# Start of the out projection's operand, two recurrence pairs later, in a one-core transformer-layer kernel on Trainium2

## The chip, the core and the metric

The kernel runs on one core of one Trainium2 chip. The core's engines each run a queue of their own in order: TensorE (PE; its weight loads are listed apart as PEld), VectorE (DVE), ScalarE (ACT), GpSimd (POOL) and SyncE (SP). In this kernel SP issues nearly all DMA transfers; the transfers themselves run on 16 DMA engines shared by all queues. The metric is the device time of one execution in microseconds (us), as the median of several runs. One more execution is recorded by the hardware profiler; it has a time of its own.

## The reference

One layer on 2048 tokens of width 1024, all in fp32. Cut to what matters here:

```python
u = rms_norm(h, g_mix_pre)
z = u @ w_in                                     # 1024 -> 2816 columns
qa, ka, va, qh, fh, ih, gh = split(z)
ya = swa_with_sinks(qa, ka, va, sinks)           # sliding-window attention, 8 heads of 64
yh = hgrn2(qh, fh, ih, gh, lb, onorm)            # gated recurrence, 4 heads of 128
y  = concatenate([ya, yh]) @ w_out               # the out projection
h  = h + rms_norm(y, g_mix_post)
y  = cross_attention(rms_norm(h, g_x_pre), rms_norm(mem, g_mem), wq_x, wk_x, wv_x, wo_x)
h  = h + rms_norm(y, g_x_post)                   # mem: 256 tokens
y  = (silu(u @ w_gate) * (u @ w_up)) @ w_down    # u = rms_norm(h, g_ffn_pre)
h  = h + rms_norm(y, g_ffn_post)
```

## The kernel before, in words

**Arithmetic.** A matrix product in fp32 is made of three faster matmuls. Each operand is split in a high and a low part: ACT (or POOL) copies it to the rounded type (L987 in `split2`), DVE subtracts the copy from the original (L990). Then come high by high, high by low and low by high (L156 to L158 in `mm3`, L1131 to L1133 in `products`). So no weight can be used by PE before one load, one copy and one subtraction have ended.

**Stages.** `mix` (L194 on) holds the first quarter of the kernel. After a first block of the in projection it makes generators and calls `next` on them in turn, so that their work lies side by side:

- `cols` is the in projection of the second half of the tokens, one column of 128 outputs for each `next`: load the weights, split them, 48 matmuls of 128x512, an activation on ACT (L706, L708) and DVE (L713), and a store to `z_d`. The last four columns are those of the gate `gh`.
- `swa` is the attention, one pair of chunks (128 tokens) for each `next`; it writes `y_d`.
- `pairs` is the recurrence for pairs 8 to 15, staggered over ten yields: `hgrn_front` loads `k`, `qq`, `kk` and `v` from `z_d` and does the products L886, L897 and L902 (the last two are transposes on PE), `hgrn_state` carries the state `W` (L913, L915), `hgrn_out` (L925) loads the gate `sg` and makes the output, and `hgrn_last` stores it to `y_d`. The tile `v` has one buffer: the next pair's `v` is loaded when the transposes L902 of this one's have read it.
- `fold` is `fold_cross` (L272 on), in 32 steps. It first loads and normalises `mem` and transposes it (L124); then eight columns of wk, eight rows of wq (each result `x` is stored to `qk_d`), eight columns of wv, and wo in eight pieces (L348 to L350, results to `vo_d`). Each step loads 512 KB of weights into a tile `raw`, of which there are a few, and splits it on ACT and DVE into `whi` and `wlo`.
- `phases` runs the large products that follow, as a list of jobs. Job 0 is the out projection, with `w_out` as its operand `T` and `y_d` as the streamed operand `S` (tiles `sraw`). Its first eight steps are a prologue: each loads one half of a 512x512 block of `w_out`, 512 KB, into a tile `z` (two buffers, the same as those of the in projection's results) and splits it to `T` with one L987 and one L990 of 128x1024. Eight halves are the whole of `w_out`. The first products of job 0 follow when the fold has ended.

**Order.** The program fixes what depends on what; a scheduler that simulates the engines then decides the order within each engine's queue, starting from the order in which the work is written. `queued` (L438 on) restricts it: what is issued under it may not be put ahead of the instructions that it is given. `traced` (L433) finds the last instruction written so far for one engine.

**The place of the change.** Before, both last columns of the in projection are finished (L238 and L239) before the fold begins. Two fold steps follow. Then a loop takes the nine remaining yields of `pairs` (L245 to L249), with two fold steps after each, and from the second to the ninth it takes one half of `w_out` each. The last twelve fold steps (L250 and L251) stand alone.

Of the kernel before, what the change touches and what calls it, by code (L numbers as in the profile page):

```python
# [48 lines left out]
class Layer:  # L49
# [144 lines left out]
    def mix(self):  # L194
        tc, I = self.tc, self.I
        kw = dict(reuse_waits="tile")
        with contextlib.ExitStack() as left:
            def pool(name, at, **k):
                return at.enter_context(tc.tile_pool(name=name, bufs=1, **k, **kw))

            self.mc = pool("mc", left)
            self.r_x = self.cst.tile([P, NT], F32, name="r_x")
            with (
                tc.tile_pool(name="t1", bufs=3, **kw) as self.ts,
                tc.tile_pool(name="t2", bufs=3, **kw) as self.tb,
                tc.tile_pool(name="s1", bufs=2, side="right", **kw) as self.st_pool,
                contextlib.ExitStack() as at,
            ):
                self.banks(at, "ps1", **MOST)
                self.raws = 3  # L210
                u = self.in_first()
            self.banks(left, "ps2", **FOUR)
            self.hg = pool("hg", left)
            self.wp = pool("wp", left)
            self.io = pool("io", left)
            with tc.tile_pool(name="sw", bufs=1, side="right", **kw) as self.sw:
                self.zero_tiles()
                swa = self.swa(range(NT), lambda n: "st" if n < NPB else "sth")
                hgrn = self.hgrn(range(NPB), "h")
                cols = self.in_proj(1, u)  # L220
                next(cols)
                for _ in range(NPB + 1):
                    next(swa)
                    next(hgrn)
                    next(cols)
                for _ in hgrn:
                    pass
                self.out_sums, side = self.sums("out_s", self.w_out, 4, lambda: self.io_tile("u"), lambda: self.io_tile("x"))
                side = side()
                next(side)  # L230
                pairs = self.hgrn(range(NPB, NT), "gt")
                for i, _ in enumerate(swa, NPB + 2):
                    next(cols)
                    if i == NT + 1 - 0:
                        next(pairs)
                    for _ in range(4):
                        next(side, None)
                for _ in cols:  # L238
                    pass  # L239
            phases = self.phases(self.jobs(), None, lambda: self.io_tile("z"))  # L240
            with tc.tile_pool(name="xp", bufs=1, side="right", **kw) as self.xp:
                fold = self.fold_cross()
                for _ in range(2):
                    next(fold)
                for i, _ in enumerate(pairs, 1):  # L245
                    for _ in range(2):
                        next(fold)
                    if 2 <= i < 10:
                        next(phases)  # L249
                for _ in fold:  # L250
                    pass  # L251
            left.close()
            with (
                tc.tile_pool(name="t3", bufs=3, **kw) as self.ts,
                tc.tile_pool(name="t4", bufs=3, **kw) as self.tb,
                tc.tile_pool(name="s3", bufs=2, side="right", **kw) as self.st_pool,
                contextlib.ExitStack() as at,
            ):
                self.banks(at, "ps3", **MOST)
                self.raws = 4  # L260
                for _ in phases:
                    pass
# [1528 lines left out]
```

## Time and profile before

| | us |
|---|---|
| median of 3 runs | 2552.73 |
| lowest and highest run | 2552.61, 2555.01 |
| the profiled execution's own time | 2550.01 |
| its span (first to last instruction) | 2548.3 |
| PE busy | 2504.8 (98%) |
| DVE busy | 1792.1 (70%) |
| ACT busy | 1261.6 (50%) |
| POOL busy | 364.6 (14%) |

How to read it: the span is what the profile's rows divide up; the profiled execution's own time has 1.7 us more around it. An engine's busy time counts its instructions, not what it waits for. Groups and timelines name an instruction by engine, line, operation and `output<-inputs`; `[2.59 <-DMA v<-z_d]` behind a row says that the engine stood idle for 2.59 us before it and that a DMA into `v` from `z_d` ended the wait. An `x` and a number count instructions that a row stands for; matmuls overlap, so such a row's length is not their sum. Windows give the busy time of each engine in a stretch, then the TensorE clock that was granted (1.00 is full speed), the mean busy share of the 16 DMA engines and the bytes they moved; shares can come out slightly above 1.

### The profile page before, as it was taken

The numbers are of one execution on the slowest core, as the hardware profiler recorded it, in microseconds if no ns is written. First come the engines' busy times: TensorE is split into PE (matmuls) and PEld (weight loads), VectorE is DVE, ScalarE is ACT, GpSimd is POOL, SyncE is SP. The second block draws the span as 40 slices with busy tenths as digits, with TensorE's granted clock in tenths as the row PEclk, the third lists the DMA queues.
The fourth block names the chain that finished last, engine by engine and source line by source line (L and its number), as shares of the span: only waits on it lengthen the run. The fifth ranks groups of instructions, "written<-read, shape, count | busy, mean of one in ns | idle before, by whom it ended". The sixth has DMA issues, their size and how long they took to land.

```text
span 2548.3 us, 34324 instructions
## 1 busy us (share of the span) xinstructions
PE 2504.8 (98%) x12006; PEld 2092.8 (82%) x12006; DVE 1792.1 (70%) x2871; ACT 1261.6 (50%) x2635; POOL 364.6 (14%) x540
## 2 busy tenths in 40 slices
PE   9999999999999999999999999999999999999998
PEld 8878888877997778878878888888888888878886
DVE  8885488987556989988876555576566557574766
ACT  5553466655555566566753333353333335443543
POOL 4231234321311112102200000000000000000022
PEclk9999999999999999999999999999999999999999
DMA  6455655865887996867954522254465434564786
GB/s 201 146 165 178 192 154 170 230 204 146 259 292 275 316 335 189 274 206 226 333 200 146 177 91 87 74 203 148 160 210 195 144 117 159 180 188 106 228 177 151
DMA packets 387885, 486.33 MB, mean 191 GB/s; under 512 B 22272, under 2 KB 283392, under 8 KB 387712
## 3 DMA queue, kind: packets, MB, share of 16 engines
q1 hardware_dynamic: 381664, 462.12, 55.9%
q0 software_dynamic: 6048, 22.02, 5.0%
q8 instruction: 94, 1.54, 0.2%
q14 instruction: 79, 0.65, 0.1%
HBM read 317.34 MB, written 166.72 MB: 190 GB/s over the span
## 4 chain that ended last, share of the span: by engine, by line
PE 51%; DVE 2%; DMA 1%; issue 1%; ACT 1%; POOL 0%; SPq 0%; DVEq 0%; POOLq 0%; ACTq 0%
PE psm L1133 17%; PE psm L1131 17%; PE psm L1132 17%; DVE T L990 0%; DVE S L990 0%; ACT junk L1504 0%; PE pss L1390 0%; DMA out_dram<-row 0%; DMA row<-d_s 0%; DMA row<-in_w_down_dram 0%; DMA u_d<-row 0%; DMA sraw<-in_w_gate_dram 0%; DVE sum L1106 0%; ACT S L987 0%; ACT T L987 0%
## 5 line engine op out<-in xcount | busy, mean ns | idle before, releaser
L1131 PE MATMUL psm<-T,S 128*128 128x512 f32 x2680 | 1034.1, 390 | 13.3 <-ACT part L1146 7.2
L1132 PE MATMUL psm<-T,S 128*128 128x512 f32 x2680 | 1042.3, 390 | 4.0 <-DVE T L990 3.9
L1133 PE MATMUL psm<-T,S 128*128 128x512 f32 x2680 | 1029.4, 389 | 4.1 <-DVE S L990 4.1
L1131 PEld LDWEIGHTS psm<-T,S 128*128 128x128 f32 x2680 | 503.0, 188 | 125.9 <-ACT part L1146 11.9
L1132 PEld LDWEIGHTS psm<-T,S 128*128 128x128 f32 x2680 | 503.2, 188 | 110.5 <-DVE T L990 7.3
L1133 PEld LDWEIGHTS psm<-T,S 128*128 128x128 f32 x2680 | 503.1, 188 | 110.6 <-DVE S L990 6.3
L987 ACT ACTIVATE S<-sum 128x512 fp32r<-128x512 f32 (+1 forms) x370 | 224.0, 620 | 371.5 <-PE psm L1133 267.3
L990 DVE TENSOR_TENSOR S<-sraw,S 128x512 fp32r<-128x512 f32 (+1 forms) x315 | 211.5, 679 | 218.8 <-ACT S L987 215.8
L1146 ACT ACTIVATE part<-psm 128x512 f32<-128x512 f32 x285 | 168.6, 596 | 251.9 <-PE psm L1133 230.9
L990 DVE TENSOR_TENSOR S<-sum,S 128x512 fp32r<-128x512 f32 (+1 forms) x388 | 257.4, 673 | 42.1 <-ACT S L987 38.3
L987 ACT ACTIVATE S<-sraw 128x512 fp32r<-128x512 f32 (+1 forms) x300 | 184.7, 618 | 110.8 <-PE psm L1133 106.0
L1537 POOL DMA_DIRECT2D y_d<-row x16 | 14.1, 879 | 1077.9 <-DVE row L1721 1027.6
L990 DVE TENSOR_TENSOR T<-row,T 128x1024 fp32r<-128x1024 f32 (+1 forms) x112 | 131.0, 1183 | 30.2 <-ACT T L987 29.2
L157 PE MATMUL psg<-u,whi 128*128 128x512 f32 x320 | 128.3, 401 | 0.0
L158 PE MATMUL psg<-u,wlo 128*128 128x512 f32 x320 | 127.6, 399 | 0.0
L156 PE MATMUL psg<-u,whi 128*128 128x512 f32 x320 | 127.5, 399 | 0.0
L1504 ACT ACTIVATE junk<-row 128x512 f32<-128x512 f32 x160 | 99.6, 624 | 40.6 <-DVE row L1526 20.6
L987 ACT ACTIVATE T<-row 128x1024 fp32r<-128x1024 f32 (+1 forms) x112 | 113.3, 1031 | 7.5 <-DMA row<-d_s 4.3
L1672 DVE TENSOR_TENSOR row<-psm,part 128x512 f32<-128x512 f32 x66 | 43.7, 687 | 66.9 <-PE psm L1133 66.9
L1681 DVE TENSOR_TENSOR part<-psm,part 128x512 f32<-128x512 f32 x66 | 43.8, 687 | 60.1 <-PE psm L1133 59.8
L1721 DVE TENSOR_TENSOR row<-psm,part 128x512 f32<-128x512 f32 x72 | 49.1, 688 | 49.5 <-PE psm L1133 49.4
L814 ACT ACTIVATE S<-S,w_mn 128x256 f32<-128x256 f32 (+1 forms) x128 | 63.0, 496 | 29.6 <-DVE w_mn L810 29.2
(363 smaller groups left out, 3562.2 us busy)
## 6 DMA issues: line engine op xcount, KB each, us to landing
sraw<-in_w_gate_dram SPq DMA_DIRECT2D x44, 512.0 KB, 3.6
sraw<-in_w_up_dram SPq DMA_DIRECT2D x44, 512.0 KB, 3.7
hid_d<-row SPq DMA_DIRECT2D x44, 512.0 KB, 2.7
sraw<-hid_d SPq DMA_DIRECT2D x32, 512.0 KB, 4.2
sraw<-in_w_in_dram SPq DMA_DIRECT2D x44, 256.0 KB, 4.0
z_d<-pair SPq DMA_DIRECT2D x20, 512.0 KB, 3.4
raw<-in_w_in_dram SPq DMA_DIRECT2D x20, 512.0 KB, 4.8
z_d<-z SPq DMA_DIRECT2D x20, 512.0 KB, 4.0
```

The source lines that it names most:

```text
L156: nc.tensor.matmul(ps, ah, bh, start=(i == 0), stop=False)
L157: nc.tensor.matmul(ps, ah, bl, start=False, stop=False)
L158: nc.tensor.matmul(ps, al, bh, start=False, stop=(i == n - 1))
L814: nc.scalar.activation(s[:, r, o:], s[:, r, o:], AF.Exp, bias=mn[:, i:i + 1], scale=-1.0, accum_out=den[:, i:i + 1])
L987: self.nc.scalar.activation(hi, raw, AF.Copy)
L990: self.nc.vector.tensor_tensor(lo, raw, f32(hi), ALU.subtract)
L1131: nc.tensor.matmul(ps, s[:, 0, k, :], t[:, 0, k, :], start=st, stop=False, **kw)
L1132: nc.tensor.matmul(ps, s[:, 0, k, :], t[:, 1, k, :], start=False, stop=False, **kw)
L1133: nc.tensor.matmul(ps, s[:, 1, k, :], t[:, 0, k, :], start=False, stop=sp, **kw)
L1146: nc.scalar.activation(t, ps, AF.Copy)
L1504: self.nc.scalar.activation(junk, a, AF.Square, scale=float(D) ** -0.5, accum_out=to)
L1721: nc.vector.tensor_tensor(d, a, b, ALU.add)
```

## The change

It lies in `mix` alone:

```diff
-                for _ in cols:
-                    pass
             phases = self.phases(self.jobs(), None, lambda: self.io_tile("z"))
             with tc.tile_pool(name="xp", bufs=1, side="right", **kw) as self.xp:
                 fold = self.fold_cross()
-                for _ in range(2):
-                    next(fold)
+                engines = [getattr(mybir.EngineType, e) for e in ("SP", "Activation", "DVE")]
+                left_over = [0] * 8
+
+                def prologue():
+                    if left_over:
+                        left_over.pop()
+                        with self.queued(*(self.traced(e) for e in engines)):
+                            next(phases)
+
+                next(cols)
+                next(fold)
+                for _ in cols:
+                    pass
+                next(fold)
                 for i, _ in enumerate(pairs, 1):
                     for _ in range(2):
                         next(fold)
-                    if 2 <= i < 10:
-                        next(phases)
+                    if i >= 4:
+                        prologue()
                 for _ in fold:
-                    pass
+                    prologue()
+                assert not left_over
```

Three things differ. The halves of `w_out` are taken from the fourth to the ninth turn of the loop over the pairs (six of them), and after the first two of the twelve fold steps that follow (two more). Each half is written under `queued`, behind the last instruction written so far on SP, ACT and DVE. And the in projection's last column is written after the fold's first step (the memory's part and the first column of wk), no longer before it; the second-last column and the second fold step keep their places around them.

## The prediction, made before the changed kernel was run

> **What bounds the kernel now.** I began with the head of the page and the chain of waits.
>
> ```profile
> span 2548.3 us, 34324 instructions
> PE 2504.8 (98%) x12006; PEld 2092.8 (82%) x12006; DVE 1792.1 (70%) x2871; ACT 1261.6 (50%) x2635; POOL 364.6 (14%) x540
> ```
>
> PE is busy for 98% of the span, so 2548.3 − 2504.8 = 43.5 us of idle PE is all that a new order can win, plus whatever PE loses to a lower clock. The change adds and removes no arithmetic; it only moves work between about 590 and 774 us. So I asked for PE's waits in that stretch (line waiting, releaser: total us, times, longest).
>
> ```profile
> PE pst L902 <- DMA v<-z_d: 2.6, 1, 2.6
> PE pst L902 <- ACT whi L126: 1.1, 1, 1.1
> PE psh L849 <- DVE ptl L844: 1.0, 1, 1.0
> PE psg L897 <- DVE W L915: 0.8, 2, 0.5
> PE pst L925 <- ACT atz L888: 0.7, 1, 0.7
> PE pss L349 <- DVE wlo L990: 0.3, 1, 0.3
> PE pss L348 <- DVE kv L304: 0.2, 1, 0.2
> ```
>
> They add to 6.7 us. The largest is the load of `v` for the second pair; PE's timeline (start, us, instruction, idle before) and that of SP, which issues the loads in order, show why:
>
> ```profile
> 623.84 0.60 PE L902 MATMUL pst<-ident,v 128*128 128x128 f32 x4
> ...
> 630.78 1.04 PE L902 MATMUL pst<-ident,v 128*128 128x128 f32 x4 [2.59 <-DMA v<-z_d]
> 631.61 1.49 PE L886 MATMUL psg<-qq,k 128*128 128x192 f32 x4
> 633.21 1.09 PE L897 MATMUL psg<-ident,kk 128*128 128x128 f32 x4
> ...
> 645.88 0.81 PE L886 MATMUL psg<-qq,k 128*128 128x192 f32 x4
> 649.79 0.60 PE L897 MATMUL psg<-ident,kk 128*128 128x128 f32 x4
> ```
> ```profile
> 616.97 1.26 SPq L75 DMA_DIRECT2D z<-in_w_out_dram  x2
> ...
> 624.74 1.25 SPq L75 DMA_DIRECT2D z<-in_w_out_dram  x2
> 626.04 0.59 SPq L75 DMA_DIRECT2D v<-z_d  x1
> ```
>
> `v` has one buffer. It is free when the transposes of 623.84 are done (624.4), but SP first issues a half of `w_out` (two loads into `z`) and reaches `v` at 626.04. PE then stands for 2.59 us, and the same instructions take longer afterwards than at 645 to 650. The windows (length, busy us by engine, then granted clock, DMA share and GB/s) say the same, and show the fold's end:
>
> ```profile
> 630.00:640.00 10.00, 9.08 (x61) 8.23 (x62) 6.45 (x10) 6.47 (x18) 3.37 (x5) 0.83 0.98 281
> ```
> ```profile
> 725.00:735.00 10.00, 10.00 (x87) 10.00 (x86) 6.50 (x8) 7.01 (x17) 1.20 (x2) 1.00 0.83 258
> 735.00:745.00 10.00, 10.00 (x86) 10.00 (x86) 5.33 (x7) 3.58 (x6) 0.00 (x0) 1.00 1.08 346
> 745.00:755.00 10.00, 9.46 (x63) 8.00 (x62) 8.22 (x13) 7.78 (x13) 0.00 (x0) 1.00 1.04 398
> 755.00:765.00 10.00, 10.00 (x44) 7.84 (x43) 4.60 (x4) 7.19 (x11) 0.00 (x0) 1.00 0.98 347
> 765.00:775.00 10.00, 10.00 (x45) 8.08 (x44) 2.95 (x3) 5.90 (x10) 0.00 (x0) 1.00 0.51 204
> ```
>
> From 735 to 765 us the DMA engines are full while PE is fed without a gap worth naming. Two stretches, two limits: a load's place in SP's queue at 626 us, the rate of DMA at 735 to 765 us.
>
> **The moved halves, at their old place.** Eight halves of `w_out`, 512 KB each, are loaded (L75), copied by ACT (L987) and subtracted by DVE (L990):
>
> ```profile
> L75 SPq DMA_DIRECT2D z<-in_w_out_dram x12: 499/603/2971, 617.0 to 656.0; - x12
> L987 ACT ACTIVATE T<-z x8: 1057/1060/1063, 622.4 to 662.6; 128x1024 fp32r<-128x1024 f32 x8
> L990 DVE TENSOR_TENSOR T<-z,T x8: 1207/1226/1470, 623.5 to 664.2; 128x1024 fp32r<-128x1024 f32 x8
> ```
>
> In the changed order the second pair's `k`, `qq` and `v` follow each other on SP, and the loads of five more pairs come before the first half. So `v` can go at 624.4, not 626.04. How long it takes is read from the issues of 610 to 662 us (engine, form, count, size, median us to landing):
>
> ```profile
> z<-in_w_out_dram SPq DMA_DIRECT2D x4, 512.0 KB, 6.9
> k<-z_d SPq DMA_DIRECT2D x3, 256.0 KB, 4.0
> v<-z_d SPq DMA_DIRECT2D x3, 256.0 KB, 4.6
> ```
>
> 624.4 + 4.6 = 629.0; PE needs it at 630.78 − 2.59 = 628.2. That leaves a wait of 0.8 us; with `k`'s 4.0 it is 0.2. I take 0.6, since less is in the queue. Gain 2.0. The slow clock is worth (1.04 − 0.60) + (1.49 − 0.81) + (1.09 − 0.60) = 1.6 us, which the window's (1 − 0.83) × 9.08 = 1.5 confirms. I let this cost vanish with the long wait. First term: −3.6, bounds 0 (the single buffer keeps `v` as late as it is) and −4.2.
>
> [...]
>
> **ACT and DVE relieved.** From 622 to 664 us they lose 8 × 1.06 = 8.5 and 8 × 1.23 = 9.8 us of work. PE's waits on `atz`, `W` and `whi` (0.7 + 0.8 + 1.1 = 2.6 us) end on ACT or DVE; the rows don't say how many of them the splits caused, and I take a third. Second term −0.8, bounds −2.6 and +1.1: at their new place the splits can make one wait as long as the longest of these.
>
> **The last gate column beside the fold's first step.** Its 48 matmuls keep their engine and number; the memory's loads, norms and eight transposes come ahead of them. Its weights are loaded later, the first step's earlier. What lies at that place is the wait of 1.0 us on `ptl` (592 us), which neither load releases. Term 0; bounds −1.0 (the new neighbours fill it) and +2.6 (a weight late by as much as `v` was).
>
> **The halves at their new place.** By the changed order three halves go between the stores of wq's results, beside the last pairs, and five follow the last of wq's stores, two of them ahead of the last two wv columns, two between the loads of the first token blocks and one before the fifth piece of wo, in SP's queue:
>
> ```profile
> 734.02 0.57 SPq L78 DMA_DIRECT2D qk_d<-x  x1
> ...
> 743.20 5.02 SPq L75 DMA_DIRECT2D raw<-in_wo_x_dram  x2
> ```
> ```profile
> 754.51 0.50 PE L349 MATMUL pss<-wlo,kv 128*128 128x512 f32 x1 [0.29 <-DVE wlo L990]
> ...
> 774.30 0.39 PE L1131 MATMUL psm<-T,S 128*128 128x512 f32 x1
> ```
> ```profile
> 740.86 1.06 ACT L987 ACTIVATE whi<-raw 128x1024 fp32r<-128x1024 f32 x1 [1.60 <-DMA raw<-in_wv_x_dram]
> ...
> 765.23 1.06 ACT L987 ACTIVATE whi<-raw 128x1024 fp32r<-128x1024 f32 x1 [0.74 <-DMA raw<-in_wo_x_dram]
> ```
>
> The stretch from 725 to 765 moves (258 + 346 + 398 + 347) × 10 us = 13.5 MB; five halves add 2.62 MB. At its own mean, 337 GB/s, that takes 7.8 us more; if all of it ran at the 398 GB/s of its best window, 16.1 MB take 40.5 us and it costs 0.5. ACT already waits for `raw` at 740.86 and 765.23, and PE for `wlo` at 754.51, so the splits are just in time: the weights have perhaps 1 us to spare (765.23 + 1.06 + 1.23 = 767.5 against its use about two steps of (774.30 − 754.51) / 7 = 2.8 us before 774.30, that is 768.7). Nor is there room in SP's queue: a `z` buffer is busy for 6.9 + 1.06 + 1.23 = 9.2 us, so with two the third and fourth of the five can be issued only 9.2 us after 734, at 743 or later, where SP would hold back the wo loads of 743.20. I take +4.0, between 0.5 and 7.8, near the middle since rate and spare time both count. Five copies and five subtractions (5.3 and 6.1 us) fit into ACT's and DVE's idle time there, and cost nothing unless late data makes them stand ahead of `whi`. `T` itself isn't late: the last half is split before the wo pieces end, and PE first needs one at 774.30.
>
> [...]
>
> **Later jobs.** Their splits and waits change order only a little; what PE waits for from 774 to 1300 us:
>
> ```profile
> PE psm L1133 <- DVE S L990: 4.1, 4, 1.6
> PE psm L1131 <- ACT S L987: 3.9, 3, 1.7
> PE psm L1132 <- DVE T L990: 3.9, 6, 1.4
> ```
>
> 11.9 us in all; nothing says which way they go. Term 0, bounds ±2 (a sixth of it).
>
> **Sum.** −3.6 − 0.8 + 0 + 4.0 + 0 = −0.4 us. The profiled execution took 2550.01 us (1.7 around its span) and would take 2549.6; it is 2.7 below the median of the runs, 2552.73, so the median becomes 2552.3. About 0.2%, 5.1 us, is what a measurement of this kernel can tell from no change.
>
> **Rivals.**
> *The fold's end takes the halves without harm* (faster). For it: PE waited only 0.3 us at wo, DMA reached 398 GB/s, and after 765 us its share falls to 0.51. Against it: that room lies behind the last load PE waits for. The sum is then −3.6 − 0.8 + 0.5 = −3.9, and with the early terms most of the way to their bounds −4.2 − 1.7 − 0.5 = −6.4: 2546.3 to 2548.8, likely 2547.5.
>
> *The wo loads queue behind the halves and PE starves at the fold's end* (slower). One mechanism: from the moment a half waits for its `z` buffer on SP, each wo load behind it is late by the rest of the 9.2 us, and the DMA then works the 2.62 MB ahead of them. It decides if the waits at L349 and L350 (wo's matmuls) add to over 4 us. Price: 7.8 by DMA, about 2.5 for SP held from 743.2 (the third and fourth half's 0.6 us each and the landing of what follows them), 1.6 for a clock that falls as it did at 631; less 4.4 gained: +7.5, so 2560.2; from 2557 on where half of the queue's cost hides.
>
> *The stall doesn't go* (the change doesn't do what it says). `v`'s single buffer and a landing of over 6 us leave most of the 2.59 us and the slow clock; only 0.5 of the first term is gained: −0.5 − 0.8 + 4.0 = +2.7, 2555.4.
>
> **How the numbers follow.** My forecast, 2552.3, has a chance of 0.36, with an own range of 2549 to 2556; halves absorbed 0.25; starved 0.26; stall stays 0.13. Faster by over 5.1 us (below 2547.6): half of the absorbed case and a sliver more where the early stretch gives its bounds too, 0.21 in all. Slower by over 5.1 (above 2557.8): nine tenths of the starved case and a little of the last two, 0.28. Within: 0.51. The range reaches into both cases, 2546.5 to 2560.5, and leaves out some 0.07 below and 0.11 above.
>
> **What would show it.** Right: no wait on `v` over 1 us and a clock of 1.00 from 630 to 640; several new waits at L348 to L350 on `wlo` or `whi`, 3 to 5 us in all, with DMA full to nearly 770; job 0 beginning at about the time it began. If job 0 begins 4 us earlier, the tail absorbed the halves; if over 5 us later, it starved. Wrong altogether if PE's time changes after 1300 us, or between 590 and 620.

## The result, and the profile after

| | before | changed |
|---|---|---|
| median, us | 2552.67 (8 runs) | 2559.57 (8 runs) |
| lowest to highest | 2549.82 to 2555.01 | 2557.71 to 2562.35 |
| profiled execution, us (span) | 2550.01 (2548.3) | 2562.35 (2560.6) |

The ratio is 1.0028, with a 95% interval of 1.0019 to 1.0037: slower, by about 7 us. The profiled execution of the changed kernel is the longest of its eight, so the two profiles lie 12.3 us apart where the medians lie 6.9 apart. Of all the runs in this document one, of e7, took 3126.36 us at a granted clock of 0.752, where every other had at least 0.994, and e7's time below is the median of its other seven.

The head of the page and PE's waits of 0.5 us or more from 590 us to the start of job 0, of the changed kernel (behind `mix` its line numbers are 11 higher: L908 is L897 of before, L913 is L902, L359 is L348, L998 is L987, L1142 is L1131):

```profile
span 2560.6 us, 34333 instructions
...
PE 2509.6 (98%) x12006; PEld 2096.0 (82%) x12006; DVE 1792.5 (70%) x2871; ACT 1262.7 (49%) x2635; POOL 365.8 (14%) x540
```
```profile
PE psh L359 <- DVE kv L315: 2.9, 1, 2.9
PE pss L359 <- ACT whi L998: 2.6, 1, 2.6
PE pss L156 <- ACT whi L126: 1.9, 1, 1.9
PE pss L156 <- ACT whi L998: 1.3, 1, 1.3
PE pss L158 <- DVE wlo L1001: 0.8, 1, 0.8
PE pss L156 <- DVE mT L127: 0.7, 1, 0.7
PE pss L360 <- DVE wlo L1001: 0.5, 1, 0.5
PE psg L908 <- DVE W L926: 0.5, 1, 0.5
```

The wait on `v` is gone. The load of `v` goes out at 621.37, right behind the transposes of 620.74 that free its buffer (623.84 before), and the transposes of 626.35 find it there. All the long waits are new, and all end on ACT or DVE work that belongs mostly to the fold (L126 splits wq's rows, L314 and L315 copy and split a column of wv's result, L359 to L361 are wo's matmuls). To see when the time changes hands, take marks that both kernels pass in the same sequence: the transposes of `kk` of the first pair (at 590 us) and of the last one, and job 0's first matmul. PE's timeline of before and then of the changed kernel:

```profile
590.54 0.60 PE L897 MATMUL psg<-ident,kk 128*128 128x128 f32 x4
...
707.65 0.60 PE L897 MATMUL psg<-ident,kk 128*128 128x128 f32 x4
```
```profile
590.15 0.66 PE L908 MATMUL psg<-ident,kk 128*128 128x128 f32 x4 [0.27 <-ACT atz L899]
...
620.74 0.60 PE L913 MATMUL pst<-ident,v 128*128 128x128 f32 x4
...
626.35 0.60 PE L913 MATMUL pst<-ident,v 128*128 128x128 f32 x4
...
700.71 0.60 PE L908 MATMUL psg<-ident,kk 128*128 128x128 f32 x4
...
708.88 0.39 PE L156 MATMUL pss<-kv,whi 128*128 128x256 f32 x1 [1.89 <-ACT whi L126]
...
743.82 0.39 PE L156 MATMUL pss<-mT,whi 128*128 128x256 f32 x1 [1.27 <-ACT whi L998]
745.08 0.38 PE L158 MATMUL pss<-mT,wlo 128*128 128x256 f32 x1 [0.76 <-DVE wlo L1001]
...
755.87 0.50 PE L359 MATMUL psh<-whi,kv 128*128 128x512 f32 x1 [2.94 <-DVE kv L315]
759.39 0.80 PE L359 MATMUL pss<-whi,kv 128*128 128x512 f32 x1 [2.55 <-ACT whi L998]
771.65 0.50 PE L360 MATMUL pss<-wlo,kv 128*128 128x512 f32 x1 [0.52 <-DVE wlo L1001]
...
782.46 0.39 PE L1142 MATMUL psm<-T,S 128*128 128x512 f32 x1
```

The pairs' stretch (first to last `kk`) takes 707.65 − 590.54 = 117.1 us before and 110.6 after: 6.5 us gained. The fold's end (last `kk` to job 0) takes 774.30 − 707.65 = 66.7 before and 81.8 after: 15.1 us lost. Job 0 begins 8.2 us later than before, though the first mark was passed 0.4 us earlier.

The windows of the changed kernel (columns as before):

```profile
630.00:640.00 10.00, 10.00 (x86) 10.00 (x85) 5.66 (x8) 4.62 (x15) 4.33 (x5) 1.00 0.84 247
...
700.00:710.00 10.00, 7.77 (x66) 7.38 (x64) 3.98 (x7) 4.31 (x9) 1.14 (x2) 1.00 0.85 236
710.00:720.00 10.00, 10.00 (x73) 9.99 (x74) 4.88 (x8) 4.59 (x15) 1.93 (x3) 0.83 0.58 193
...
740.00:750.00 10.00, 7.97 (x65) 7.57 (x64) 7.71 (x10) 6.48 (x10) 0.00 (x0) 1.00 1.10 308
750.00:760.00 10.00, 4.50 (x21) 3.17 (x21) 5.94 (x9) 5.55 (x8) 0.00 (x0) 0.91 1.04 363
760.00:770.00 10.00, 10.00 (x35) 7.95 (x34) 4.10 (x4) 6.70 (x10) 0.00 (x0) 0.75 0.97 365
```

Where 630 to 640 us had a clock of 0.83 it now has 1.00 and a busy PE. But 700 to 710 and 740 to 760 have idle PE, and a slower clock follows each: 0.17 × 10.0 + 0.09 × 4.5 + 0.25 × 10.0 = 4.6 us, an estimate from the windows. The waits after 700.71 add 1.89 + 0.34 (a second one on `whi` at 710) + 1.27 + 0.76 + 2.94 + 2.55 + 0.52 = 10.3 us; before had 0.5 there. Together 10.3 + 4.6 − 0.5 = 14.4 of the 15.1 us.

Why PE waits is read from ACT, DVE and SP of the changed kernel:

```profile
707.29 1.06 ACT L998 ACTIVATE T<-z 128x1024 fp32r<-128x1024 f32 x1 [4.08 <-DMA z<-in_w_out_dram]
708.25 0.58 ACT L126 ACTIVATE whi<-pss 128x512 fp32r<-128x512 f32 x1
...
753.17 1.06 ACT L998 ACTIVATE T<-z 128x1024 fp32r<-128x1024 f32 x1 [0.95 <-DMA z<-in_w_out_dram]
754.13 0.37 ACT L314 ACTIVATE kv<-psh 128x256 fp32r<-128x256 f32 x1
...
758.28 1.06 ACT L998 ACTIVATE whi<-raw 128x1024 fp32r<-128x1024 f32 x1 [2.08 <-DMA raw<-in_wo_x_dram]
```
```profile
754.26 1.23 DVE L1001 TENSOR_TENSOR T<-z,T 128x1024 fp32r<-128x1024 f32 x1 [1.24 <-ACT T L998]
755.40 0.42 DVE L315 TENSOR_TENSOR kv<-psh,kv 128x256 fp32r<-128x256 f32 x1
```
```profile
732.27 0.34 SPq L78 DMA_DIRECT2D qk_d<-x  x1
732.66 2.27 SPq L75 DMA_DIRECT2D z<-in_w_out_dram  x3
...
735.62 1.76 SPq L75 DMA_DIRECT2D raw<-in_wv_x_dram  x2
...
741.84 2.74 SPq L75 DMA_DIRECT2D z<-in_w_out_dram  x3
...
746.45 4.97 SPq L75 DMA_DIRECT2D raw<-in_wo_x_dram  x3
```

Two things. At 707 us ACT stands 4.08 us for a half that hasn't landed, and the copy of `whi` (L126), for which PE waits, stands behind it on the same engine; at 753 it is the copy of `kv` (L314), and on DVE its subtraction (L315) stands behind that of the half. And on SP the halves are issued ahead of weights: the second load for wo goes at 746.45 (743.20 before), the fifth at 760.62 (754.49), and ACT waits for a wo load until 758.28. The DMA engines didn't make up for it. One window from wq's last store to job 0, before and then changed; both hold the same loads and stores, but for the five halves:

```profile
734.02:774.30 40.28, 39.74 (x238) 34.32 (x237) 20.61 (x25) 24.18 (x39) 0.00 (x0) 1.00 0.91 326
```
```profile
732.27:782.46 50.19, 42.14 (x232) 35.60 (x230) 27.78 (x32) 30.20 (x45) 0.00 (x0) 0.93 0.91 301
```

The share was 0.91 and stays so, and the stretch grew by 9.9 us. At the 326 GB/s of before the 2.62 MB of five halves alone are 8.0 us: they were paid with time.

### The profile page after: what moved, and what is told of

It is laid out like the page before. It is cut to its first block, busy times and chain, and to the rows that moved or that the text cites. A ratio compares the mean times of both kernels' runs of the same rounds, so it can differ in the third digit from the quotient of the medians.

```text
span 2560.6 us, 34333 instructions
## 1 busy us (share of the span) xinstructions
PE 2509.6 (98%) x12006; PEld 2096.0 (82%) x12006; DVE 1792.5 (70%) x2871; ACT 1262.7 (49%) x2635; POOL 365.8 (14%) x540
## 4 chain that ended last, share of the span: by engine, by line
PE 51%; DVE 2%; ACT 1%; issue 1%; DMA 1%; POOL 0%; SPq 0%; DVEq 0%; POOLq 0%; ACTq 0%
PE psm L1142 17%; PE psm L1144 17%; PE psm L1143 17%; DVE T L1001 1%; DVE S L1001 0%; ACT junk L1515 0%; PE pss L1401 0%; ACT T L998 0%; DMA row<-in_w_down_dram 0%; DMA out_dram<-row 0%; DMA row<-d_s 0%; DMA u_s<-row 0%; DVE sum L1117 0%; ACT S L998 0%; DVE row L1645 0%
## 5 line engine op out<-in xcount | busy, mean ns | idle before, releaser
L1142 PE MATMUL psm<-T,S 128*128 128x512 f32 x2680 | 1034.5, 391 | 14.5 <-ACT part L1157 7.3
L1142 PEld LDWEIGHTS psm<-T,S 128*128 128x128 f32 x2680 | 503.4, 188 | 127.5 <-ACT part L1157 11.9
L1144 PEld LDWEIGHTS psm<-T,S 128*128 128x128 f32 x2680 | 503.6, 188 | 112.3 <-DVE S L1001 8.1
L998 ACT ACTIVATE S<-sum 128x512 fp32r<-128x512 f32 (+1 forms) x370 | 223.8, 620 | 378.8 <-PE psm L1144 278.9
L998 ACT ACTIVATE S<-sraw 128x512 fp32r<-128x512 f32 (+1 forms) x300 | 184.8, 617 | 107.7 <-PE psm L1144 103.6
L998 ACT ACTIVATE T<-row 128x1024 fp32r<-128x1024 f32 (+1 forms) x112 | 113.3, 1030 | 7.7 <-DMA row<-d_s 4.8
L1526 POOL TENSOR_TENSOR q_v<-q_s 128x2 f32<-128x2 f32 x39 | 16.8, 431 | 426.0 <-ACT junk L1515 426.0
```

The costliest lines, as they stand in the source:

```text
L998: self.nc.scalar.activation(hi, raw, AF.Copy)
L1142: nc.tensor.matmul(ps, s[:, 0, k, :], t[:, 0, k, :], start=st, stop=False, **kw)
L1144: nc.tensor.matmul(ps, s[:, 1, k, :], t[:, 0, k, :], start=False, stop=sp, **kw)
```

## The experiments

Each ran five rounds against the kernel before. The table reads every kernel by the marks above (us, from each kernel's profiled execution): first to last `kk`, last `kk` to job 0, their sum, and job 0 to the end.

| | pairs | fold's end | sum | rest | ratio to before, 95% interval |
|---|---|---|---|---|---|
| before | 117.1 | 66.7 | 183.8 | 1774.0 | |
| changed | 110.6 | 81.8 | 192.3 | 1778.1 | 1.0028 [1.0019, 1.0037] |
| e1 column only | 119.7 | 69.4 | 189.1 | 1774.1 | 1.0005 [0.9995, 1.0015] |
| e2 halves only | 110.8 | 80.8 | 191.6 | 1782.9 | 1.0030 [1.0018, 1.0042] |
| e3 no load | 110.9 | 78.3 | 189.2 | 1777.7 | 1.0004 [0.9995, 1.0014] |
| e4 v, two buffers | 117.5 | 67.8 | 185.3 | 1778.0 | 0.9992 [0.9983, 1.0001] |
| e5 few bytes | 110.1 | 74.6 | 184.7 | 1778.2 | 0.9988 [0.9978, 0.9998] |
| e6 split later | 110.4 | 83.4 | 193.8 | 1775.0 | 1.0023 [1.0015, 1.0032] |
| e7 earlier in turn | 122.2 | 72.7 | 194.9 | 1779.4 | 1.0037 [1.0024, 1.0050] |
| e8 earlier, split later | 110.7 | 74.2 | 184.9 | 1773.6 | 1.0006 [0.9995, 1.0016] |
| e9 two per turn | 121.3 | 65.0 | 186.3 | 1773.5 | 1.0006 [0.9997, 1.0015] |
| e10 two, SP only | 119.6 | 68.7 | 188.3 | 1772.4 | 1.0006 [0.9998, 1.0015] |
| e11 two, old column | 122.1 | 66.4 | 188.4 | 1777.4 | 1.0015 [1.0006, 1.0024] |
| e12 mixed | 122.6 | 66.7 | 189.3 | 1776.7 | 1.0011 [1.0001, 1.0021] |

Three cautions for the table. The last time column scatters by itself: over these kernels it lies between 1772.4 and 1782.9 us, and e4, which differs from before only in a buffer of `v`, has 1778.0 where that has 1774.0. So 4 us between two profiles of that part tell nothing, and the changed kernel's +4.1 there isn't put down to the change. Next, a profile is one execution: e8's is the shortest of its eleven, 6.7 us below their median, those of e3 and of the changed kernel are their longest. What the sums say is therefore held against the ratios, which come from all runs; before's own median in these rounds lay between 2552.59 and 2554.86 us. Last, the marks part the same work in most kernels, but not in all. Between the first and the last `kk` PE has 793 to 797 matmuls in the others, 782 in e8, 810 and 811 in e9 and e11, and 826 in e12. At about 0.12 us for one of the fold's (an estimate from their spacing) some 1.7 us of the pairs' work is counted at the fold's end in e8; as much of the fold's end is counted among the pairs in e9 and e11, and 3.5 us of it in e12. The sums don't change by that.

**e1, column only.** The changed kernel without the queueing:

```diff
-                        with self.queued(*(self.traced(e) for e in engines)):
-                            next(phases)
+                        next(phases)
```

> The changed kernel without the queueing of the halves; the scheduler then loads them at their old place beside the second to fifth pairs (the order of all loads is that of a kernel in which only the last gate column is moved). If the loss comes from the halves at the fold's end (theory): 2550 to 2555 us, job 0 begins within 2 us of 774, the long wait on v is there again or smaller. If moving the column costs (rival): 2557 us or more, with new waits before 640 us.

2556.22 us against 2554.86, between the two expectations; job 0 begins at 778.6 us, later than the theory had it. The halves are loaded from 617 to 657 us, where the kernel before has them: writing them two turns later has no effect, and the queueing alone moves them. The stall stays and has another name. DVE and PE of this kernel:

```profile
629.82 0.17 DVE L287 TENSOR_SCALAR gx<-gx 128x8 f32<-128x8 f32 x1 [2.06 <-DMA gx<-in_g_x_pre_dram]
```
```profile
630.73 0.55 PE L156 MATMUL psh<-mT,whi 128*128 128x256 f32 x1 [2.47 <-DVE mT L127]
```

DVE stands for `gx`, a load of 4 KB, and the split `mT` behind it keeps PE waiting. The pairs' stretch is 119.7, the fold's end 69.4: nearly all of the loss at the fold's end belongs to the queued halves.

**e2, halves only.** Both last columns before the fold, as in the kernel before; the halves as changed:

```diff
+                for _ in cols:
+                    pass
             phases = self.phases(self.jobs(), None, lambda: self.io_tile("z"))
...
-                next(cols)
-                next(fold)
-                for _ in cols:
-                    pass
-                next(fold)
+                for _ in range(2):
+                    next(fold)
```

> The halves queued later as in the changed kernel, both gate columns before the fold as in the kernel before. Theory: 2557 to 2562 us, PE waits of 6 to 10 us in all between 740 and 775 us and one of some 2 us near 705, job 0 begins 6 to 9 us later than before. Rival (the column's move costs): 2553 us or less.

2562.38 us. 110.8 and 80.8 us, the changed kernel's stretches to within 1 us: the halves do all of it, the gain among the pairs too, and moving the column is worth nothing beside them.

**e3, no load.** From the third half on `get` in `phases` gives back one of the first two tiles and loads nothing, so `T` isn't `w_out`:

```diff
+                if tile is prologue and len(stale) >= 2:
+                    stale.append(0)
+                    return stale[len(stale) % 2][:, :c]
```

> The changed kernel with the loads of the third to eighth half left out: their copies and subtractions stay and read the tiles of the first two. If the 3 MB and the waits for them make the loss (theory): 2544 to 2548 us, no PE wait over 1 us between 740 and 775. If the copies and subtractions make it by their own time, standing between those of the fold (rival): 2555 us or more.

2556.32 us, as a time in the rival's range; but before had 2554.86 in these rounds, and a loss of 1.5 us is neither the theory's gain nor as much as the rival had. The second half is still loaded, ACT stands 5.26 us for it and PE 3.08; and with the loads gone the scheduler put token loads ahead of the last wv columns, where PE waits 2.38 us at 755 though no half is loaded there. The run doesn't separate the theories.

**e4, two buffers for v.** In the kernel before:

```diff
-        v = get(new("v"), C_IH)
+        v = get(new("v", 2), C_IH)
```

> The kernel before with a second buffer for v and nothing else changed. If the place of v's load behind the halves made the stall of 2.59 us and the slow clock after it: the wait on v is gone, 2548 to 2550 us. If the load is late for another reason (DMA full, the data not yet in memory): the wait stays or goes to another tile, 2551 to 2554 us.

0.9992, not clear of 1. PE's wait on `v` is gone, and the next transposes wait in its place:

```profile
626.61 0.49 PE L902 MATMUL pst<-ident,v 128*128 128x128 f32 x3
...
630.61 0.63 PE L897 MATMUL psg<-ident,kk 128*128 128x128 f32 x4 [2.86 <-issue]
```

117.5 us among the pairs, as before. So the single buffer of `v` was not what cost. What the next transposes wait for isn't shown: the row names no releaser, and SP issued their `kk` at 590 us already.

**e5, few bytes.** The changed kernel; the loads of the third to eighth half take 64 of 512 columns, so `T` isn't `w_out` here either:

```diff
+                if tile is prologue and len(stale) >= 2:
+                    t = stale[len(stale) % 2]
+                    stale.append(t)
+                    jobs[n][0](t[:, :c, 0:64], i, j, a, c, 64)
+                    return t[:, :c]
```

> The changed kernel with an eighth of the bytes in the loads of the third to eighth half (64 of 512 columns; the rest of T is made from stale data). The queueing, the copies and the subtractions stay. From the last product of wq to job 0 the kernel before takes 44.2 us, the changed one 54.9. If the bytes in the full DMA stretch make the loss (theory): 44 to 47 us, no wait over 1 us there, time within 3 us of before. If the place of the copies and subtractions in ACT's and DVE's order makes it (rival): 50 us or more.

2552.46 us, 0.9988: in the medians all of the loss is gone, and more. From wq's last product to job 0 it takes 47.2 us, at the edge of what the theory expected. The fold's end falls from 81.8 to 74.6 us with the copies and subtractions still there: about half of the 15.1 us goes with the bytes. ACT's standing for the last five halves (4.0 us in the changed kernel) goes with them, so this run alone doesn't part the two. What is left holds a PE wait of 3.07 us at 711, behind ACT's 5.25 us for the second half, which is loaded whole in this run; from 745 us on there remain waits of 1.92 and 0.38.

**e6, split later.** In the prologue each half is split after the next one's load is written:

```diff
                 half(-1, prologue)
-                split(len(steps))
+                if i:
+                    split(len(steps))
                 yield
+            split(len(steps))
```

> The changed kernel with each half's copy and subtraction written one half after its load, so that ACT need not stand still for the load; bytes and queueing stay. If ACT's standing in order for the halves, with the fold's copies behind it, makes most of the loss: the wait near 705 us gone, the stretch from wq's last product to job 0 at 46 to 49 us, 2550 to 2555 us. If the bytes alone make it: that stretch stays above 52 us and the time near 2558.

2559.81 us, 83.4 at the fold's end, 54.3 from wq's last product to job 0: the second branch of the expectation. ACT's standing for halves falls to 2.4 us in all (11.4 in the changed kernel), and nothing is won, because another load is late and another engine stands for it. DVE and PE:

```profile
725.26 0.75 DVE L955 SCALAR_TENSOR_TENSOR sg<-psg,onorm,sg 128x512 f32<-128x512 f32 x1 [3.79 <-DMA sg<-z_d]
```
```profile
726.66 0.58 PE L158 MATMUL psh<-kv,wlo 128*128 128x256 f32 x1 [4.06 <-DVE wlo L127]
```

**e7, earlier in the turn.** The changed kernel with one half in each of the first eight turns, ahead of the fold's two steps:

```diff
+                    if i >= 1:
+                        prologue()
                     for _ in range(2):
                         next(fold)
-                    if i >= 4:
-                        prologue()
```

> The halves still queued, but one in each of the first eight turns and ahead of the turn's two fold steps: the loads then stand one behind each pair's loads, from the second pair to the wv columns, and only the last is within the stretch of full DMA. If the full stretch makes the loss: wq's last product to job 0 in 44 to 47 us, 2546 to 2553 us. If a queued half costs wherever it stands (ACT in order for its load): waits of 1 to 3 us with a slower clock between 645 and 730, 2555 us or more.

2564.74 us, with the highest ratio of all. The loads now stand behind each pair's; from wq's last product to job 0 it takes 46.9 us, as the theory had it, but the pairs' stretch 122.2, as the rival had it: both costs are there. Each half makes ACT stand; the view of the tile `z` gives the sum and the number (of before, then of this kernel):

```profile
  DMA z<-in_w_out_dram: 17.5, 8
```
```profile
  DMA z<-in_w_out_dram: 32.4, 8
```

The longest, on ACT and then on PE:

```profile
662.99 1.06 ACT L998 ACTIVATE T<-z 128x1024 fp32r<-128x1024 f32 x1 [7.61 <-DMA z<-in_w_out_dram]
663.96 0.25 ACT L899 ACTIVATE atz<-psg 64x128 f32<-64x128 f32 x1
```
```profile
664.26 1.12 PE L954 MATMUL psg<-ident,on 128*128 128x128 f32 x4 [2.06 <-ACT atz L899]
```

**e8, both.** e7's place and e6's later split:

```diff
+                if i:
+                    split(len(steps))
...
+                    if i >= 1:
+                        prologue()
                     for _ in range(2):
                         next(fold)
```

> The two edits together (one half behind each pair, its copy and subtraction one half later). Both theories: no wait of PE over 1.2 us from 640 to 775, wq's last product to job 0 in 44 to 47 us; 2545 to 2551 us, faster than the kernel before. If moving the halves can gain nothing (rival, the stall on v being no loss that can be won): 2552 us or more.

2556.71 us, 1.0006. ACT stands 4.2 us for halves. Of e7's excess among the pairs hardly anything is left (110.7, or some 112.3 with the matmuls that lie behind the mark), and the sum, 184.9, is 7.4 below the changed kernel's. With e6 and e7 this closes a square: too many bytes at the fold's end with a free ACT is slow (193.8), a better place with an ACT that stands is slow (194.9), and only the two together are not (184.9). The ratios bear it out with smaller steps, e6 4 us and e7 8 us above e8. It is no faster than before, against the expectation: the last halves stand among wv's loads, and a wait of 1.85 on `wlo` at 724 us and a clock of 0.83 after it stay.

**e9, two per turn.** Two halves in each turn from the second to the fifth, one ahead of each fold step, with e6's later split:

```diff
                     for _ in range(2):
+                        if i >= 2:
+                            prologue()
                         next(fold)
-                    if i >= 4:
-                        prologue()
```

> The halves queued two in each turn from the second to the fifth, each ahead of a fold step, with copy and subtraction written one half later: all loads stand after the stall on v and before the stretch of full DMA. If both costs are as found (bytes in the full stretch; ACT in order for a load), neither is left: 588 to 774 us in at most 181 us from the second-last gate column to job 0 (before: 181.1, changed: 190.2), no wait above 1.2 us after 640; 2545 to 2551 us with before at 2553. If any queued half costs: new waits over 1.5 us between 650 and 700 and 2555 us or more.

2553.25 us, 1.0006. The last half is issued at 704 us, and the fold's end is as short as before (65.0, or some 66.7 with the matmuls ahead of the mark); the pairs pay instead (121.3, or 119.6): two halves stand ahead of a pair's `v`, and ACT stands 6.60 us for one at 675. The expectation of a gain was wrong.

**e10, queued on SP only.** As e9, and:

```diff
-                engines = [getattr(mybir.EngineType, e) for e in ("SP", "Activation", "DVE")]
+                engines = [getattr(mybir.EngineType, e) for e in ("SP",)]
```

> As the run before it, but queued behind SP's last instruction alone, so that the scheduler places copies and subtractions on ACT and DVE as it likes. If ACT's order is what the queueing spoils: as good or up to 3 us better than the run before it. If the scheduler puts the copies ahead of data that is not there: waits on whi or atz of 1 to 3 us, and 2 to 5 us slower.

2553.84 us, 1.0006, the same as e9. Where ACT's and DVE's queues are left to the scheduler they come out no better.

**e11, two per turn, old column.** As e9, with the fold's first steps as in e2:

```diff
-                next(cols)
-                next(fold)
-                for _ in cols:
-                    pass
-                next(fold)
+                for _ in range(2):
+                    next(fold)
```

> As the run before the last, with the last gate column back before the fold. If the column's move is worth nothing by itself: within 2 us of that run. If it wins the early stretch: 2 to 5 us slower, with waits near 590 to 640 that the other lacks.

2556.12 us, 1.0015: 2.9 us above e9 and so in the second branch, but the intervals overlap. The stretches differ by 0.8 and 1.4 us. Inconclusive beyond what e2 shows.

**e12, mixed.** One, one, one, two, two, one in the first six turns, later split:

```diff
                     for j in range(2):
+                        if j < [0, 1, 1, 1, 2, 2, 1, 0][min(i, 7)]:
+                            prologue()
                         next(fold)
```

> Halves queued one, one, one, two, two and one in the first six turns, each ahead of a fold step, copy and subtraction one half later: no two halves stand together ahead of a pair's v, and the loads of the fold's end have the order of the kernel before. If the costs found are all there is: 178 to 181 us from the second-last gate column to job 0, no wait above 1.2 us from 640 to 775, ratio to before 0.998 to 0.9995. If every place of a half takes some load's turn in a DMA that is nearly full (rival): waits of 1 to 3 us on pairs' loads or the fold's weights remain, ratio 1.000 to 1.002.

2557.88 us, 1.0011. 122.6 among the pairs and 66.7 at the fold's end; with the 30 matmuls that lie ahead of the mark here it is rather 119 and 70, so both stretches pay. PE waits 2.91 us for `atz` at 700.69, behind ACT's 5.59 us for a half. The rival of this expectation holds. No arrangement of whole loads tried here beats the kernel before.

## Why the prediction was wrong

The forecast was no change (−0.4 us); the time rose by 6.9. The second rival, halves queued ahead of the wo loads with PE starving at the fold's end, gave 2560.2, and 2559.57 was measured. That its number is so close is in part luck. It took a loss of 7.8 + 2.5 + 1.6 = 11.9 us less a gain of 4.4; the profiles show 15.1 less 6.5. Its sign of decision was over 4 us of waits at L349 and L350; the wo matmuls wait 2.94 + 2.55 + 0.52 = 6.0, but at the first two of the three products (L359 and L360, which are L348 and L349), and only the 0.52 at one that it named. ACT's standing at 707 us wasn't in it.

**The step that failed** is "The halves at their new place", where I took +4.0 between 0.5 and 7.8. It measured +15.1, far outside the bounds. Three parts were missing:

- The rate. I took the bytes at the mean rate and let some 4 us of them hide. From wq's last store to job 0 the rate fell, from 326 to 301 GB/s, and none hid: 40.3 us became 50.2. e5 gives back 7.2 us of the fold's end when most bytes go.
- ACT in order. I costed the copies at nothing "unless late data makes them stand ahead of `whi`", and gave that condition no price and no chance. It came true for the second half at 707 us already, before the full stretch. The square of e6, e7 and e8 shows that this and the bytes each spoil the sum where the other is mended: by 9 to 10 us in the profiles (193.8 and 194.9 against 184.9), by 4 and 8 us in the ratios. How much of the 15.1 us is each one's alone stays open. At 753 us the half's copy and subtraction also took time of their own, about 1 us each, ahead of `kv`.
- The clock. Some 4.6 us of slow clock followed the new waits: 0.83 after 1.89 and 0.34 us, 0.91 and then 0.75 after 2.94 and 2.55 us. I had counted it on the gain's side (1.6) and in the rival, not in this term.

**The stall on `v`.** Right in kind: the wait is gone and the clock is 1.00 from 630 to 640. With the relief of ACT and DVE I gave 3.6 + 0.8 = 4.4; the pairs' stretch gained 6.5. But the reason was too narrow. I named a place in SP's queue and the single buffer; e4 gives `v` a second buffer and PE waits at `kk`, in e1 at `mT`, with the stretch at 117 to 120 us. And the changed order frees `v` 3 us earlier than the 624.4 that I took as given. What cost there was the eight halves within 40 us, with their copies right behind; with all but one of them later the stretch is 110 to 111 in the changed kernel, e2, e3, e5 and e6 alike, and one behind each pair with its copy later costs little (e8).

**The last gate column.** Term 0, and e2 against the changed kernel gives 0.7 us. Right, as far as single profiles tell.

**Later jobs.** Term 0 ± 2. The profiles show +4.1, which e4 shows to be within the scatter of one profile. Not settled, and not needed for the sum: 8.2 us at job 0 against 6.9 in the medians.

The range held the time, but only because it reached into the rivals, and because the pairs' gain was 2.1 us larger than I took. What misled was the term's likeliest value, set near the middle of two bounds that were both bounds of DMA alone.

## What to carry to other kernels

The prefetch that was moved to another stretch was paid there (15.1 us at the fold's end against 6.5 gained among the pairs). Where you move one, first read the new stretch's DMA share over its whole length, and where it is as high as here (0.91), price every byte at the rate it already has (326 GB/s here, 8.0 of the 9.9 us by which that stretch grew), with nothing hidden, as the least that it costs. Then go through what stands behind the prefetch's first use on its engine: here the copies of halves that were late held up the copies behind them, and PE, which waited for those, paid a part of the standing (1.89 us for 4.08 in the changed kernel, 2.06 for 7.61 in e7, 2.91 for 5.59 in e12) and a slow clock after it: for some 3.5 us from 710 us on in the changed kernel and some 5 us from 664 on in e7 its matmuls of 256 columns took 0.41 us instead of 0.28, and for some 3.5 us from 701 on in e12 two of 128 columns took 0.64 instead of 0.39. Where a scheduler orders the queues, look at the resulting order before costing a moved line: here the move in the source left the halves where they were, and the queueing constraint moved them.

## What the runs showed of the hardware

In the kernel before, matmuls of split operands with 256 columns came 0.12 us apart (at 640 us); two products of 192 unsplit columns (L886, 645.88 us), four matmuls in the trace, took 0.81 us together. The clock fell after idle times of about 2 us in several kernels: 0.83 after 1.89 + 0.34 us in the changed one, 0.83 after 1.85 us in e8. It doesn't fall after each of them: in e7 it stayed at 1.00 after 2.23 us (712 us) and after 1.96 + 0.30 (732 us). What decides between them these runs don't show. An engine that stands isn't itself a loss: ACT stood 17.5 us for halves in the kernel before, 11.4 in the slower one. And the kernel before, always the same program, took between 2547.6 and 2560.4 us over its runs beside these experiments, so that differences under 0.1% between two kernels stayed open at five rounds each.
